# Gathering a convolution's last three rows by GpSimd, and turning them once for several tiles, in a hybrid SSD and attention layer

## The chip, the cores and the metric

The kernel runs on one core of a Trainium2 chip. The metric is the device time of one execution in microseconds (us). A core has five engines with a queue each, which is worked off in order: TensorE (PE in the profile; its weight loads are shown apart as PEld), VectorE (DVE), ScalarE (ACT), GpSimd (POOL) and SyncE (SP, which only issues DMA transfers here). ACT and POOL issue transfers as well. Engines wait for each other by semaphores.

## The reference, cut to what matters

One layer of a decoder trunk is computed for 512 prompt rows and for 8 samples of 8 rows each, 576 columns together in the kernel. After a first feed-forward block, one wide projection makes, among others, the 3072 channels `xBC`. These run through a causal depthwise convolution of four taps and SiLU, and then into the SSD scan and the attention branch's merge. Two outputs are the last three rows of the convolution's input: `conv_prompt` (3 x 3072) and `conv_sample` (8 x 3 x 3072).

```python
def causal_conv(xbc, conv_prev, conv_w, conv_b):
    L = xbc.shape[1]
    xa = jnp.concatenate([conv_prev.astype(xbc.dtype), xbc], axis=1)
    y = conv_b + sum(xa[:, j:j + L] * conv_w[j] for j in range(D_CONV))
    return jax.nn.silu(y), xa[:, L:]
```

For the prompt, `conv_prev` is zero; for the samples it comes from `state_conv`. The second value that is returned, `xa[:, L:]`, is what this document is about. The outputs are stored with a row's channels side by side, while the kernel holds channels on partitions, so that these rows have to be turned (transposed) on their way out.

## The kernel before, in words

All activations lie with 128 channels on the partitions and the 576 rows along the free dimension. Every large matrix product is made of three products of rounded halves (`mm3`, lines 207 to 215): the weights come by DMA into `stage`, ACT rounds them to `whi` (L176), and DVE or POOL subtracts to `wlo` (L177). In this part of the kernel every second subtraction goes to POOL (`share[0] = 2`). `whi` and `wlo` have four buffers, and a tile of 128 output channels uses two of each. The 576 rows are worked off in two halves of 288, each in one PSUM bank given out by `acc()`; in the convolution part that is the pool `acc` with two banks. One half is 24 matmuls of 288 columns.

`conv_tile` handles 128 of the 3072 channels. It is called 24 times, by `group_in(g)` for the four groups g: once for the group's B channels, once for C, four times for x. `group_in(0)` stands ahead of the attention branch's output projection; the groups 1 to 3 are computed beside `group_scan` of the group before, in the order that a scheduler puts the instructions in by priority and its own simulated times. `soon()` raises the priority of what is inside it.

One tile goes like this. POOL zeroes three columns of `xr` and copies the samples' old rows into it (L1156, L1157). PE computes the first half, DVE evicts it (L1161). PE computes the second half, DVE evicts its prompt columns (L1166) and its sample columns (L1168). Then PE turns the last 3 + 8 x 11 = 91 columns of `xr` into the unused columns 384 to 511 of the second half's own bank (L1174; `acc(True)` hands out the full bank), ACT copies the turned rows to `tt` (L1176), and ACT's queue issues four transfers from `tt` to the outputs: three rows of `conv_p` (L1177) and three times eight rows of `conv_s` (L1180). `tt` has one buffer.

The convolution itself is one ACT operation (L1185), three on DVE (L1187), a tanh on ACT that overwrites `xr` (L1188), and two DVE operations that write `bT`, `cT` or `xg` (L1189, L1191). `xr` has three buffers and `cv` (tag `kf`) two.

In `group_scan`, `bT` and `cT` are multiplied on PE (L1319), `xg` is turned (L1342), and `xdt` and `dk` are the operands of the scan's products (L1345, L1333, L1358). The bank tag `tr` (two banks) serves the other turns.

Of the kernel before, what the change touches and what calls it, by code (L numbers as in the profile page):

```python
# [17 lines left out]
AF = mybir.ActivationFunctionType  # L18
# [5 lines left out]
P = 128  # L24
OFFSET = 3000
D = 1024
NP = 512
NS = 64
NT = NP + NS
HT = NT // 2  # L30
B = 8
T = 8
# [3 lines left out]
CONV = 3072  # L36
# [6 lines left out]
CZ, CX, CB, CC, CDT = 0, 2048, 4096, 4608, 5120  # L43
# [46 lines left out]
def ap3(ap, offset, dims):  # L90
    return bass.AP(tensor=ap.tensor, offset=ap.offset + offset, ap=[list(d) for d in dims])


def build(ctx, tc, A, O):
    nc = tc.nc
    uid = [0]

    def tl(pool, shape, dt=F32, tag=None, bufs=None):
        uid[0] += 1
        kw = {} if bufs is None else {"bufs": bufs}  # L100
        return pool.tile(shape, dt, tag=tag, name=f"{tag}_{uid[0]}", **kw)
# [5 lines left out]
    act = nc.scalar.activation  # L107
    V = nc.vector
    G = nc.gpsimd

    constp = ctx.enter_context(pool("const"))
# [10 lines left out]
    ident = tl(constp, [P, P], tag="ident")  # L122
# [9 lines left out]
    def tr():  # L132
        return bank("tr", 2)
# [9 lines left out]
    def acc(full=False):  # L143

        wide[1] += 1
        a = wide[0]() if wide[0] and wide[1] % 2 else tl(accp, [P, 512], tag="acc")
        return a if full else a[:, :HT]
# [270 lines left out]
    with pool("h1", reuse_waits="tile") as hp:  # L418
        hts = [tl(hp, [P, NT], tag=f"h{k}") for k in range(8)]
        nrm1 = Norm(0)  # L420
        with pool("xin", side="right", reuse_waits="tile") as xi:
# [4 lines left out]
            for half in range(2):  # L426
                d = slice(half * (D // 2), (half + 1) * (D // 2))
                for c in range(5):
                    n = P if c < 4 else NS
# [5 lines left out]
            t = tr()  # L435
            nc.tensor.transpose(t[:, :8], r1, ident[:8, :8])
            V.tensor_copy(P1[:, :8], t[:, :8])
            for k in range(8):
                t = tr()
# [6 lines left out]
                t = sm()  # L446
# [5 lines left out]
            for c in range(5):  # L452
                n = P if c < 4 else NS
# [6 lines left out]
        with pool("setup2", side="right", reuse_waits="tile") as su:  # L460
            q = nc.scalar

            r1 = tl(su, [66, P], tag="r1")

            def rows(o, ap, n):
                q.dma_start(out=r1[o:o + n, :], in_=ap.rearrange("o (k p) -> (o k) p", p=P))

            rows(0, A["ffn1_norm"], 8)
            rows(8, A["mix_norm"], 8)
            rows(16, A["ffn2_norm"], 8)  # L470
            rows(24, A["ssd_norm"], 16)
            rows(40, A["conv_b"], 24)
            for i in range(2):
                q.dma_start(out=r1[64:65, i * 64:(i + 1) * 64], in_=A["q_norm"])
                q.dma_start(out=r1[65:66, i * 64:(i + 1) * 64], in_=A["k_norm"])
            t = tr()
            nc.tensor.transpose(t[:, :66], r1, ident[:66, :66])
            V.tensor_copy(P1[:, 8:], t[:, 8:66])
            V.tensor_scalar(P1[:, 40:64], t[:, 40:64], 0.5, None, ALU.mult)
            V.tensor_scalar(P1[:, 64:65], t[:, 64:65], -0.125, None, ALU.mult)  # L480
            r2 = tl(su, [96, P], tag="r2")
            q.dma_start(out=r2, in_=A["conv_w"].rearrange("o j (k p) -> (o j k) p", p=P))
            P2 = tl(constp, [P, 96], tag="P2")
            t = tr()
            nc.tensor.transpose(t[:, :96], r2, ident[:96, :96])
            V.tensor_scalar(P2, t[:, :96], 0.5, None, ALU.mult)
            r3 = tl(su, [16, 2], tag="r3")
            q.dma_start(out=r3, in_=A["d_skip"].rearrange("o (j e) -> (o j) e", e=2))
            r4 = tl(su, [16, 2, 64], tag="r4")
            V.tensor_copy(r4, r3.unsqueeze(2).to_broadcast([16, 2, 64]))  # L490
            dsk = tl(constp, [P, 16], tag="dsk")
            t = tr()
            nc.tensor.transpose(t[:, :16], r4.rearrange("j e p -> j (e p)"), ident[:16, :16])
            V.tensor_copy(dsk, t[:, :16])

            bb = tl(constp, [48, 1], tag="bb")
            behind(q.dma_start(out=bb[:32], in_=A["dt_bias"].rearrange("o h -> h o")), nrm1.insts[7])
            behind(q.dma_start(out=bb[32:48], in_=A["b_f"].rearrange("o h -> h o")), nrm1.insts[7])
            V.tensor_scalar(bb[32:48], bb[32:48], -1.0, None, ALU.mult)
            al = tl(constp, [48, 1], tag="al")  # L500
            V.memset(al, 0.0)
            behind(q.dma_start(out=al[:32], in_=A["a_log"].rearrange("o h -> h o")), nrm1.insts[7])
            act(al, al, AF.Exp)
            V.tensor_scalar(al, al, -1.0, None, ALU.mult)

            pcol = tl(su, [P, B], I32, tag="pcol")
            for b in range(B):
                q.dma_start(out=pcol[:, b:b + 1], in_=ap3(A["page_table"], b * NPG, [(1, NPG), (0, 8), (1, 1)]))
            rq = tl(su, [P, 4], tag="rq")
            q.dma_start(out=rq, in_=A["consts"][:, COFF["rq"][0]:COFF["rq"][0] + 4])  # L510
            pidx = tl(constp, [P, B, 4], I32, tag="pidx")
            pf32 = tl(su, [P, B], tag="pf32")
            V.tensor_copy(pf32, pcol)
            V.tensor_scalar(pf32, pf32, 32.0, None, ALU.mult)
            V.tensor_tensor(pidx, pf32.unsqueeze(2).to_broadcast([P, B, 4]), rq.unsqueeze(1).to_broadcast([P, B, 4]), ALU.add)
# [67 lines left out]
    win = A["w_in"][0]  # L583
# [18 lines left out]
    with pool("dtf", side="right", reuse_waits="tile") as dp:  # L602
        w = []
# [7 lines left out]
        for half in range(2):  # L611
            a = pv()
# [29 lines left out]
        for c in range(5):  # L642
            n = P if c < 4 else NS
            t = tr()
# [17 lines left out]
    with pool("att", side="right", reuse_waits="tile") as ap:  # L662
# [67 lines left out]
        for p in range(2):  # L730
            for g2 in range(0, 4, 2):
                st2 = []
                for k in range(0, 8, 4):
                    stg = tl(wp, [P, 4, 2, 2, 64], tag="stage", bufs=4)
                    for gi in range(2):
                        for e in range(2):
                            c0 = CQ + (2 * p + e) * 256 + (g2 + gi) * 64
                            nc.sync.dma_start(out=stg[:, :, gi, e, :],
                                              in_=win[k * P:(k + 4) * P, c0:c0 + 64].rearrange("(k p) c -> p k c", p=P))
# [29 lines left out]
        t = tr()  # L769
# [378 lines left out]

    XR = [P, 3 + NP + B * (T + 3)]

    def conv_tile(ct, w, prev, out):

        xr = tl(xz, XR, tag="xr", bufs=3)
        xsamp = xr[:, 3 + NP:]
        xsamp = xsamp.rearrange("p (b u) -> p b u", u=T + 3)
        G.memset(xr[:, :3], 0.0)  # L1156
        first = G.tensor_copy(xsamp[:, :, :3], prev.rearrange("p (j b) -> p b j", b=B))  # L1157
        a = acc()
        mm3(a, w, xs, 0)
        with soon():  # L1160
            V.tensor_tensor(xr[:, 3:3 + HT], a, rbc[:, hs(0)], ALU.mult)  # L1161
        a = acc(True)
        full, a = a, a[:, :HT]
        mm3(a, w, xs, 1)
        with soon():
            V.tensor_tensor(xr[:, 3 + HT:3 + NP], a[:, :NP - HT], rbc[:, HT:NP], ALU.mult)  # L1166
        with soon():
            V.tensor_tensor(xsamp[:, :, 3:], a[:, NP - HT:].rearrange("p (b t) -> p b t", t=T),  # L1168
                            rbc[:, NP:].rearrange("p (b t) -> p b t", t=T), ALU.mult)

        n = 3 + (T + 3) * B
        with soon():
            t = full[:n, 512 - P:]
            nc.tensor.transpose(t, xr[:, NP:], ident)  # L1174
            tt = tl(xz, [n, P], tag="tt", bufs=1)
            act(tt, t, AF.Copy)  # L1176
        nc.scalar.dma_start(out=O["conv_p"][0, 0, :, ct * P:(ct + 1) * P], in_=tt[:3])  # L1177
        for j in range(3):
            r = 3 + T + j
            nc.scalar.dma_start(out=O["conv_s"][0, :, j, ct * P:(ct + 1) * P], in_=tt[r:r + (T + 3) * (B - 1) + 1:T + 3])  # L1180

        m = NP + B * (T + 3)
        cv = tl(mixp, XR, tag="kf", bufs=2)
        wc = lambda j: P2[:, j * 24 + ct:j * 24 + ct + 1]
        act(cv[:, :m], xr[:, :m], AF.Identity, bias=P1[:, 40 + ct:41 + ct], scale=wc(0))  # L1185
        for j in range(1, 4):
            V.scalar_tensor_tensor(cv[:, :m], xr[:, j:j + m], wc(j), cv[:, :m], ALU.mult, ALU.add)  # L1187
        tanh = act(xr[:, :m], cv[:, :m], AF.Tanh)  # L1188
        V.scalar_tensor_tensor(out[:, :NP], xr[:, :NP], 1.0, cv[:, :NP], ALU.add, ALU.mult)  # L1189
        samples = lambda v: v[:, NP + 3:].rearrange("p (b u) -> p b u", u=T + 3)[:, :, :T]  # L1190
        last = V.scalar_tensor_tensor(out[:, NP:].rearrange("p (b t) -> p b t", t=T), samples(xr), 1.0, samples(cv), ALU.add, ALU.mult)  # L1191
        convs.append((first, tanh, last))
# [3 lines left out]
    def group_in(g):  # L1196

        scT = tl(xz, [P, 6, 24], tag="scT", bufs=1)
        nc.sync.dma_start(out=scT[:, :4, :], in_=scD[:, 4 * g:4 * g + 4, :])
        nc.sync.dma_start(out=scT[:, 4:, :], in_=ap3(scD, (16 + g) * 24, [scD.ap[0], (4 * 24, 2), (1, 24)]))  # L1200
        bT = tl(xz, [P, NT], tag="bT", bufs=2)
        conv_tile(16 + g, Cols(win, CB + g * P, width=P).get(0), scT[:, 4, :], bT)
        cT = tl(xz, [P, NT], tag="cT", bufs=2)
        conv_tile(20 + g, Cols(win, CC + g * P, width=P).get(0), scT[:, 5, :], cT)
        xc = Cols(win, CX + g * 512)
        xg = tl(xz, [P, 4, NT], tag="xg", bufs=2)
        for i in range(4):
            conv_tile(4 * g + i, xc.get(i), scT[:, i, :], xg[:, i, :])
        return bT, cT, xg

    nxt = group_in(0)
# [344 lines left out]
```

## Time and profile before

| | us |
|---|---|
| median of three runs | 1865.89 |
| lowest and highest of them | 1864.46, 1866.64 |
| the profiled execution | 1864.62 |
| its span, first to last instruction | 1862.8 |

The profile is of one execution. "Busy" is the time in which an engine had an instruction in work; the matmuls are pipelined, so that two that are started 0.13 us apart last 0.29 us each in the rows. A row of the groups or of the waits names a line of the kernel, an engine, and the tile written. A suffix q (ACTq) is the engine's queue: issuing a transfer takes the queue's time and not the engine's. A wait for several semaphores is put down to the one that came last.

### The profile page before, as it was taken

Reading aid. Unit: us, or ns where it says so; the run is one execution under the profiler, and the core shown is the slowest. Engines: PE = TensorE matmul, PEld = TensorE weight load, DVE = VectorE, ACT = ScalarE, POOL = GpSimd, SP = SyncE. Lnnn points to the kernel's source line nnn. Section 1 sums busy time; section 2 is a strip of 40 time slices with the busy share of each in tenths; the row PEclk is TensorE's granted clock in tenths of the full one; section 3 lists DMA queues with packets and bytes.
Section 4 is the critical chain, followed back from the end, with each engine's and each line's share of the span. In section 5 each row is a group of like instructions: output and inputs, shape, how many; then the busy total and the mean of one; then the engine's idle time right before and its main releaser. Section 6 shows DMA issues by size and latency. Waiting matters only on the chain.

```text
span 1862.8 us, 38777 instructions
## 1 busy us (share of the span) xinstructions
PE 1827.1 (98%) x15335; PEld 1724.5 (93%) x15335; DVE 1050.9 (56%) x2281; ACT 754.9 (41%) x1571; POOL 626.4 (34%) x697
## 2 busy tenths in 40 slices
PE   8999999999999999999999999989999999999998
PEld 7999999999889888888998898878999999999998
DVE  4643334443425777776737968787676454344542
ACT  4333223333323555555426555555433333123322
POOL 0433002212322445543324544746454222002210
PEclk9999999999999999999999999999999999999999
DMA  4644443344525688775356545354473344554342
GB/s 149 163 124 136 132 140 103 114 139 138 145 72 172 194 240 246 225 226 173 91 158 184 140 126 144 108 148 135 132 226 93 118 120 128 148 146 119 108 123 65
DMA packets 297723, 269.72 MB, mean 145 GB/s; under 512 B 55068, under 2 KB 262092, under 8 KB 297388
## 3 DMA queue, kind: packets, MB, share of 16 engines
q1 hardware_dynamic: 229712, 184.16, 35.0%
q10 hardware_dynamic: 57828, 46.10, 8.0%
q0 software_dynamic: 10000, 36.97, 6.2%
q8 instruction: 121, 1.98, 0.4%
q14 instruction: 62, 0.51, 0.1%
HBM read 223.72 MB, written 38.73 MB: 141 GB/s over the span
## 4 chain that ended last, share of the span: by engine, by line
PE 87%; DVE 6%; DMA 3%; ACT 2%; issue 1%; ACTq 1%; POOL 0%; SPq 0%; DVEq 0%; POOLq 0%
PE acc L212 16%; PE acc L213 16%; PE acc L214 16%; PE pv L213 8%; PE pv L212 8%; PE pv L214 8%; PE tr L962 2%; PE tr L949 1%; PE mm L885 1%; DMA ab<-cumD 1%; DVE kf L1187 1%; PE pv L916 1%; PE pv L1358 1%; PE mm L903 1%; PE pv L1000 1%
## 5 line engine op out<-in xcount | busy, mean ns | idle before, releaser
L176 ACT ACTIVATE whi<-stage 128x512 fp32r<-128x512 f32 (+2 forms) x474 | 294.3, 622 | 696.0 <-PE acc L213 606.3
L212 PE MATMUL acc<-xh,whi 128*128 128x288 f32 x1792 | 540.9, 302 | 9.0 <-DVE xr L1161 5.6
L213 PE MATMUL acc<-xl,whi 128*128 128x288 f32 x1792 | 531.2, 296 | 0.0
L214 PE MATMUL acc<-xh,wlo 128*128 128x288 f32 x1792 | 531.2, 297 | 0.0
L177 DVE TENSOR_TENSOR wlo<-stage,whi 128x512 fp32r<-128x512 f32 (+1 forms) x373 | 271.5, 728 | 251.4 <-ACT whi L176 242.6
L212 PEld LDWEIGHTS acc<-xh,whi 128*128 128x128 f32 x1792 | 337.7, 188 | 16.5 <-DVE xr L1161 7.9
L213 PEld LDWEIGHTS acc<-xl,whi 128*128 128x128 f32 x1792 | 337.9, 189 | 1.7 <-issue 1.4
L214 PEld LDWEIGHTS acc<-xh,wlo 128*128 128x128 f32 x1792 | 337.2, 188 | 2.1 <-issue 1.5
L348 POOL TENSOR_TENSOR u<-u,s 128x288 f32<-128x288 f32 x88 | 82.1, 934 | 436.6 <-DVE u L347 378.0
L177 POOL TENSOR_TENSOR wlo<-stage,whi 128x512 fp32r<-128x512 f32 (+1 forms) x101 | 138.8, 1375 | 265.7 <-ACT whi L176 248.8
L212 PE MATMUL pv<-xh,whi 128*128 128x288 f32 (+1 forms) x720 | 213.8, 297 | 0.0
L213 PE MATMUL pv<-xl,whi 128*128 128x288 f32 (+1 forms) x720 | 212.4, 295 | 0.0
L214 PE MATMUL pv<-xh,wlo 128*128 128x288 f32 (+1 forms) x720 | 212.0, 295 | 0.0
L213 PEld LDWEIGHTS pv<-xl,whi 128*128 128x128 f32 (+1 forms) x720 | 134.5, 187 | 1.3
L212 PEld LDWEIGHTS pv<-xh,whi 128*128 128x128 f32 (+1 forms) x720 | 134.6, 187 | 0.4
L214 PEld LDWEIGHTS pv<-xh,wlo 128*128 128x128 f32 (+1 forms) x720 | 134.5, 187 | 0.2
L212 PE MATMUL pv<-hh,whi 128*128 128x288 f32 x352 | 105.7, 300 | 0.0
L213 PE MATMUL acc<-hl,whi 128*128 128x288 f32 x352 | 104.1, 296 | 0.0
L212 PE MATMUL acc<-hh,whi 128*128 128x288 f32 x352 | 104.1, 296 | 0.0
L213 PE MATMUL pv<-hl,whi 128*128 128x288 f32 x352 | 104.1, 296 | 0.0
L214 PE MATMUL acc<-hh,wlo 128*128 128x288 f32 x352 | 104.1, 296 | 0.0
L214 PE MATMUL pv<-hh,wlo 128*128 128x288 f32 x352 | 103.8, 295 | 0.0
(366 smaller groups left out, 3601.7 us busy)
## 6 DMA issues: line engine op xcount, KB each, us to landing
stage<-in_w_in_dram SPq DMA_DIRECT2D x52, 512.0 KB
stage<-in_ffn_w_up_dram SPq DMA_DIRECT2D x44, 512.0 KB
stage<-in_ffn_w_gate_dram SPq DMA_DIRECT2D x43, 512.0 KB
stage<-in_ffn_w_down_dram SPq DMA_DIRECT2D x40, 512.0 KB
h<-in_state_ssm_dram SPq DMA_DIRECT2D x64, 256.0 KB
hTD<-hT ACTq DMA_DIRECT2D x32, 256.0 KB
pb<-pastD SPq DMA_DIRECT2D x32, 256.0 KB
ab<-cumD SPq DMA_DIRECT2D x32, 256.0 KB
```

The costliest lines, as they stand in the source:

```text
L176: act(hi, view, AF.Copy)
L177: e.tensor_tensor(lo, view, hi.bitcast(F32), ALU.subtract)
L212: mm(out, lhsT=hi, rhs=a, start=first and i == 0, stop=False)
L213: mm(out, lhsT=hi, rhs=b, start=False, stop=False)
L214: end = mm(out, lhsT=lo, rhs=a, start=False, stop=last and i == n - 1)
L348: G.tensor_tensor(u, u, sil[half], ALU.mult)
L885: mm(s[:, :n], lhsT=q, rhs=ks[2 * self.p + e][:, :n], start=hl == 0, stop=hl == 1)
L903: nc.tensor.transpose(t[:, j * P:(j + 1) * P], lt[:, j * P:(j + 1) * P], ident)
L916: mm(self.ob[o:o + 32, i * P:(i + 1) * P], lhsT=vtok[j][:, v0:v0 + 32], rhs=self.pts[e][:, j * P:(j + 1) * P], start=j == 0, stop=j == i)
L949: nc.tensor.transpose(t[:, i * P:(i + 1) * P], kk[:, i, p * P:(p + 1) * P], ident)
L962: mm(s[kv * 32:(kv + 1) * 32, :], lhsT=self.q(kv), rhs=self.kT[kv // 2], start=True, stop=True)
L1000: mm(ob[kv * 32:(kv + 1) * 32, :64], lhsT=self.pt[:, i * P + kv * 32:i * P + (kv + 1) * 32], rhs=vv[:, i, kv * 64:(kv + 1) * 64], start=jq ...
```

## The change

The turn in each tile is replaced by a gather. A new tile `tail` (one buffer, up to 108 columns of 128 partitions) takes, for each of n channel tiles, the three last prompt columns and the 24 last sample columns (three of each of the eight samples). Two copies on POOL write them, raised in priority. When the n tiles have been gathered, `store3` turns `tail` at once into a `tr` bank, ACT copies it to `tt`, and two transfers on ACT's queue write all of the n tiles' rows. Within a group n is 2 for B and C, which lie 4 x 128 channels apart in the output, and 4 for the x tiles. Over the kernel, 24 turns, 24 copies on ACT and 96 transfers become 8, 8 and 16, and 48 copies on POOL are new. The turn and the copy are no longer raised in priority. The second half's bank is taken as any other half's. In the set-up, two one-column constants, `bb` and `al`, become the two columns of one tile `ba`.

```diff
-            bb = tl(constp, [48, 1], tag="bb")
+            ba = tl(constp, [48, 2], tag="ba")
+            bb, al = ba[:, :1], ba[:, 1:]
...
-            al = tl(constp, [48, 1], tag="al")
...
+    def rows3(n):
+
+        return tl(xz, [P, 108], tag="tail", bufs=1)[:, :27 * n]
+
+    def store3(tail, n, ct, step):
+
+        t = tr()
+        nc.tensor.transpose(t[:27 * n, :P], tail, ident)
+        tt = tl(xz, [108, P], tag="tt", bufs=1)
+        act(tt[:27 * n], t[:27 * n, :P], AF.Copy)
+        for name, r0, rows in (("conv_p", 0, 3), ("conv_s", 3 * n, 24)):
+            nc.scalar.dma_start(out=ap3(O[name], ct * P, [(step * P, n), (CONV, rows), (1, P)]), in_=tt[r0:r0 + rows * n])
+
-    def conv_tile(ct, w, prev, out):
+    def conv_tile(ct, w, prev, out, last3):
...
-        a = acc(True)
-        full, a = a, a[:, :HT]
+        a = acc()
         mm3(a, w, xs, 1)
...
-        n = 3 + (T + 3) * B
+        tail, i, n = last3
         with soon():
-            t = full[:n, 512 - P:]
-            nc.tensor.transpose(t, xr[:, NP:], ident)
-            tt = tl(xz, [n, P], tag="tt", bufs=1)
-            act(tt, t, AF.Copy)
-        nc.scalar.dma_start(out=O["conv_p"][0, 0, :, ct * P:(ct + 1) * P], in_=tt[:3])
-        for j in range(3):
-            r = 3 + T + j
-            nc.scalar.dma_start(out=O["conv_s"][0, :, j, ct * P:(ct + 1) * P], in_=tt[r:r + (T + 3) * (B - 1) + 1:T + 3])
+            G.tensor_copy(tail[:, 3 * i:3 * i + 3], xr[:, NP:NP + 3])
+            G.tensor_copy(tail[:, 3 * n + 24 * i:3 * n + 24 * (i + 1)].rearrange("p (b j) -> p b j", j=3), xsamp[:, :, T:])
...
         bT = tl(xz, [P, NT], tag="bT", bufs=2)
-        conv_tile(16 + g, Cols(win, CB + g * P, width=P).get(0), scT[:, 4, :], bT)
+        tail = rows3(2)
+        conv_tile(16 + g, Cols(win, CB + g * P, width=P).get(0), scT[:, 4, :], bT, (tail, 0, 2))
         cT = tl(xz, [P, NT], tag="cT", bufs=2)
-        conv_tile(20 + g, Cols(win, CC + g * P, width=P).get(0), scT[:, 5, :], cT)
+        conv_tile(20 + g, Cols(win, CC + g * P, width=P).get(0), scT[:, 5, :], cT, (tail, 1, 2))
+        store3(tail, 2, 16 + g, 4)
         xc = Cols(win, CX + g * 512)
         xg = tl(xz, [P, 4, NT], tag="xg", bufs=2)
+        tail = rows3(4)
         for i in range(4):
-            conv_tile(4 * g + i, xc.get(i), scT[:, i, :], xg[:, i, :])
+            conv_tile(4 * g + i, xc.get(i), scT[:, i, :], xg[:, i, :], (tail, i, 4))
+        store3(tail, 4, 4 * g, 1)
```

## The prediction

> **What bounds the kernel now.** I read the page first: busy shares, then the chain that ended last.
>
> ```profile
> span 1862.8 us, 38777 instructions
> PE 1827.1 (98%) x15335; PEld 1724.5 (93%) x15335; DVE 1050.9 (56%) x2281; ACT 754.9 (41%) x1571; POOL 626.4 (34%) x697
> ...
> PE 87%; DVE 6%; DMA 3%; ACT 2%; issue 1%; ACTq 1%; POOL 0%; SPq 0%; DVEq 0%; POOLq 0%
> ```
>
> PE is busy 98% of the span and 87% of the chain, so time can only be won as PE work taken away, PE idle time closed, or PE clock regained. The windows view then says where the idle time lies; its columns are length, busy microseconds of PE, PEld, DVE, ACT and POOL, the granted clock and the DMA share.
>
> ```profile
> 0.00:885.00 885.00, 873.66 (x7918) 814.08 (x7919) 456.15 (x1097) 366.29 (x765) 272.56 (x315) 1.00 0.55 160
> 885.00:1275.00 390.00, 372.42 (x2997) 340.02 (x2996) 289.04 (x560) 197.06 (x443) 182.89 (x209) 0.99 0.49 136
> 1275.00:1862.00 587.00, 581.07 (x4425) 570.36 (x4423) 305.75 (x625) 191.59 (x363) 170.92 (x174) 1.00 0.43 129
> ```
>
> All 24 convolution tiles run from 885 to 1275 us. PE idles 390.0 - 372.4 = 17.6 us there, about half of the whole span's idle time, and only there is the clock below full. Next, whom PE waits for from 890 us to 1275 us (total, times, longest):
>
> ```profile
> PE acc L212 <- DVE xr L1161: 5.6, 6, 3.2
> PE pv L1358 <- DVE xdt L1345: 3.4, 3, 1.9
> PE acc L212 <- ACT tt L1176: 1.6, 4, 0.8
> PE mm L1319 <- DVE cT L1191: 1.4, 1, 1.4
> ...
> PE acc L1174 <- DVE xr L1168: 0.4, 1, 0.4
> ```
>
> The first and third rows, 5.6 + 1.6 = 7.2 us, are waits of an ordinary matmul for a free `acc` bank. To see why, I read the longest on three engines, PE, DVE and ACT in turn.
>
> ```profile
> 1232.52 0.29 PE L213 MATMUL acc<-xl,whi 128*128 128x288 f32 x1
> 1232.66 0.27 PE L1174 MATMUL acc<-ident,xr 128*91 128x128 f32 x1
> 1232.68 0.38 PE L214 MATMUL acc<-xh,wlo 128*128 128x288 f32 x1
> 1236.23 0.61 PE L212 MATMUL acc<-xh,whi 128*128 128x288 f32 x1 [3.17 <-DVE xr L1161]
> ```
> ```profile
> 1231.50 0.21 DVE L1168 TENSOR_TENSOR xr<-acc,rbc 128x64 f32<-128x64 f32 x1
> ...
> 1234.02 1.78 DVE L1187 SCALAR_TENSOR_TENSOR kf<-xr,P,kf 128x600 f32<-128x600 f32 x1 [1.36 <-ACT kf L1185]
> 1235.73 0.44 DVE L1161 TENSOR_TENSOR xr<-acc,rbc 128x288 f32<-128x288 f32 x1
> ```
> ```profile
> 1236.07 0.26 ACT L1176 ACTIVATE tt<-acc 91x128 f32<-91x128 f32 x1
> ```
>
> There are two `acc` banks. One was evicted for the convolution at 1231.71 (L1168), but the turn L1174 writes into the same bank, so it stays held until the copy L1176 ends at 1236.33. The other is held until L1161 ends at 1236.17. PE, done with its half by 1233.06, takes whichever comes free first. Without the turn in the bank it could have gone on at 1233.06.
>
> The stop costs a second time. Two windows behind it, and one behind the 1.90-us wait at 1043:
>
> ```profile
> 1236.00:1240.00 4.00, 3.77 (x10) 2.74 (x11) 4.00 (x8) 0.64 (x3) 1.49 (x3) 0.50 0.96 300
> 1240.00:1244.00 4.00, 4.00 (x25) 4.00 (x25) 1.71 (x5) 2.14 (x4) 0.15 (x1) 0.74 0.01 4
> ...
> 1043.00:1047.00 4.00, 3.63 (x31) 2.67 (x32) 3.80 (x9) 3.98 (x11) 2.16 (x4) 0.64 0.15 36
> ```
>
> The granted clock is 0.50 and 0.74 over eight microseconds: 4 x 0.50 + 4 x 0.26 = 3.0 us of PE work lost. The Trainium skill ("TensorE: Matmul & The Clock Gate", Part 1) puts the drop to half clock behind an idle window of some 3.4 us. The trace disagrees, since waits of 3.17 and 1.90 us were followed by it; by the rule the clock term below would be left out, and the forecast be 2.0 us later.
>
> **The change part by part.** First what goes. Times are as minimum/median/maximum ns.
>
> ```profile
> L1180 ACTq DMA_DIRECT2D out_dram<-tt x72: 645/652/755, 899.7 to 1270.0; - x72
> L1176 ACT ACTIVATE tt<-acc x24: 249/272/274, 899.1 to 1268.0; 91x128 f32<-91x128 f32 x24
> L1177 ACTq DMA_DIRECT2D out_dram<-tt x24: 255/262/293, 899.4 to 1268.3; - x24
> ```
>
> *Turns.* 24 become 8. The 270 ns of one overlap with their neighbours: above, L214 starts 0.02 us behind the turn where it would start 0.13 behind L213, so that the turn cost 0.03; elsewhere a 128-column turn is followed thus:
>
> ```profile
> 927.74 0.27 PE L1174 MATMUL acc<-ident,xr 128*91 128x128 f32 x1
> 927.85 0.27 PE L1342 MATMUL mm<-ident,xg 128*64 128x128 f32 x1
> ```
>
> that is 0.11 us. 16 x 0.03 to 0.11 = 0.5 to 1.8; I take **1.1 us**. The new ones turn fewer columns (54 and 108) but stream the same 128, so a kept turn costs the same.
>
> *Bank waits.* Every half's bank is now free after its evictions, and turns go to a `tr` bank. Ceiling 7.2. The nine shorter ones sum to 7.2 - 3.2 = 4.0; they are copy latency, nothing else stands behind most of them, and I take 3.0. Of the 3.2 I take 2.1, because DVE is behind there too (L1187 waits 1.36, then takes 1.78) and the next eviction stays late. Together **5.1 us**, from 0 to 7.2.
>
> *Clock.* If the 3.2 falls below the 1.90 that still halved the clock, 3.0 come back; I take **2.0**, from 0 to 3.0.
>
> *ACT's queue.* Copies: 16 x 0.27 = 4.4 us less. Issues: 24 x 0.26 + 72 x 0.65 = 53 us go; 16 new ones (12 or 6 rows, 96 or 48 rows) come at 0.26 to 0.65 each, 4 to 10 us. ACT isn't the bound; what reaches PE is one place:
>
> ```profile
> ACT whi L176 <- DMA out_dram<-tt: 5.9, 3, 3.2
> ```
> ```profile
> 1146.27 0.63 ACT L176 ACTIVATE whi<-stage 128x512 fp32r<-128x512 f32 x1 [3.19 <-DMA out_dram<-tt]
> 1146.29 0.65 ACTq L1180 DMA_DIRECT2D out_dram<-tt  x1
> 1146.98 0.70 ACT L1188 ACTIVATE xr<-kf 128x600 f32<-128x600 f32 x1
> ```
>
> ACT stands for 3.19 us, put down to these transfers, before the tanh L1188 that `cT` needs; then PE waits the 1.4 us for `cT` (row above). I take **0.7**, from 0 to 1.4. L1174's own wait for L1168, 0.4, goes too.
>
> Gains: 1.1 + 5.1 + 2.0 + 0.7 + 0.4 = **9.3 us** (ceiling 1.8 + 7.2 + 3.0 + 1.4 + 0.4 = 13.8).
>
> Now what is added: 48 small copies on POOL. The nearest rows are the same shape the other way round, and the operation on DVE that meets it most:
>
> ```profile
> L1157 POOL COPY xr<-scT x24: 200/360/827, 897.2 to 1253.3; 128x24 f32<-128x24 f32 x24
> ```
> ```profile
> L1187 DVE SCALAR_TENSOR_TENSOR kf<-xr,P,kf x72: 820/834/1882, 899.3 to 1269.8; 128x600 f32<-128x600 f32 x72
> ```
>
> The 24-column copy by that row is 0.20 to 0.83; the 3-column one I set at most as long. Taking 0.36 + 0.15 gives 24 x 0.51 = 12 us more on POOL, 183 of 390 before, so POOL has room. L1187's maximum is over twice its median, so DVE is stretched at times; if each gather holds DVE for its length, DVE loses up to 12 us in the stretch. DVE has 6% of the chain: 0.06 x 12 = 0.7; I take **1.0**, from 0 to 12.
>
> Two waits are new. The tanh L1188 overwrites `xr`, and now waits for the gather on POOL instead of the turn on PE; behind it on ACT stand later weight roundings, hence PE. Between L1168 and the tanh lie one L1185 and three L1187, 0.9 + 3 x 0.83 = 3.4 us, which cover a gather of 0.5 and one operation ahead of it. I count 0; uncovered, ACT's tanh would be late by up to the 1.3 us of the second row below, 31 us over 24 tiles, of which PE meets only what isn't hidden by its 6.4 us of matmuls a tile. And each of the 8 turns waits for the last gather, with PE's in-order queue behind it. POOL's queue is no fast one:
>
> ```profile
> POOL wlo L177 <- ACT whi L176: 124.1, 30, 9.1
> ```
> ```profile
> L177 POOL TENSOR_TENSOR wlo<-stage,whi x45: 1257/1292/3054, 887.5 to 1274.8; 128x512 fp32r<-128x512 f32 x45
> ```
>
> POOL stands 124.1 / 30 = 4.1 us at a time at the head of its queue for ACT, and a gather queued behind such a wait shares it. But the program's order places a turn on PE only where its input should be ready: the 24 old turns waited 0.4 us in all. I take 8 x 0.1 = **0.8**, from 0 to 8 x 1.8 = 14 (one weight subtraction of 1.3, the median of the second row, and one gather of 0.5).
>
> `tail` has one buffer: the first x gather waits for the B/C turn, a tile (48 matmuls x 0.13 = 6.4 us) earlier; that tile is the cover, and without it the wait is the one just bounded. `ba` merges two tiles of the set-up and adds no instruction: 0, long before 885 us.
>
> Sum: 9.3 - 1.0 - 0.8 = **7.5 us faster**. The profiled execution took 1864.6 us (span 1862.8 and 1.8 around it), 1.3 below the median of 1865.9. So 1857.1 in the profile's terms, **1858.4** beside the median.
>
> **The rivals.**
>
> *More is won.* ACT without 43 us of issues also shortens PE's `xdt` waits (3.4 us) and the slow clock behind the 1.90-us one (4 x 0.36 = 1.4 at least). For: both lie where ACT and DVE alternate. Against: the row names DVE. 13.8 - 1.8 + about 2 = 14 us: 1852.
>
> *The time comes back.* DVE is busy 289 of 390 us, and it is what most of the remaining waits name; a PE that comes earlier waits longer there. Then only the turns and a part of the first group's waits are kept: 1.1 + 2.0 - 1.8 = 1.3 us, 1864.6.
>
> *The lock.* Each gather stretches DVE work that is on the path: 9.3 - 12 = 2.7 us slower, 1868.6. For: L1187's 1882 ns. Against: DVE idles 101 us in the stretch. The Trainium skill ("SBUF — State Buffer", SBUF: two separate sides) says that a VectorE operation with two SBUF inputs and a GpSimd one that reads SBUF exclude each other for a whole instruction. L1187 is of that kind, and its spread agrees.
>
> *Slower: the late turn.* The last gather is queued behind a weight subtraction that waits for ACT, and PE stands at the 8 turns. At 1.8 us each 14 us come and 9.3 go, and at waits near 1.9 the clock halves again, some 3 us for one such place: 9.3 - 14 - 3 = 8 us slower, 1873.6. It decides from 9.3 / 8 = 1.2 us per turn. For: the 4.1-us stands on POOL. Against: the order puts turns late.
>
> That the change doesn't free the bank would be the second rival's result.
>
> **How the numbers follow.** Forecast 0.47, more 0.13, back again 0.22, lock 0.06, late turn 0.12. About 0.2% (3.7 us) is what a measurement of this kernel can tell from no change. Forecast and more give faster: 0.60. Back again and two thirds of the lock give same: 0.26. The rest gives slower: 0.14. The range runs from 1849 (a little below the fullest gain, for an order built anew) to 1869 (the lock, and a mild late turn); it leaves out about 0.15.
>
> **What would show it.** Right: in 885 to 1275 us, no wait of L212 for a copy of `tt`, those for L1161 under 2 us in all, the stretch's granted clock nearer 1.00 than its 0.99, PE's waits at 8 turns under 1 us, ACT's DMA issues on `tt` 16. Wrong: PE waiting for the POOL gather by over 1.2 us a turn, `xdt` or `cT` waits grown by what L212's lost, L1187's mean clearly longer, or PE idle time grown outside the stretch, since the order of all work is built anew.

## The result, and the profile after

| | before | after |
|---|---|---|
| median, us | 1865.18 | 1877.13 |
| lowest and highest, us | 1864.08, 1866.64 | 1876.23, 1878.5 |
| ratio, 95% interval | | 1.0064 [1.0047, 1.0082] |
| span of the profiled execution, us | 1862.8 | 1875.9 |

The change makes the kernel slower by 0.64%, some 12 us. The forecast was 1858.4 us in a range of 1849 to 1869.

The page of after, its span, busy shares and chain:

```profile
span 1875.9 us, 38712 instructions
...
PE 1827.0 (97%) x15319; PEld 1725.8 (92%) x15319; DVE 1036.3 (55%) x2281; ACT 752.7 (40%) x1555; POOL 639.4 (34%) x745
...
PE 89%; DVE 4%; DMA 3%; ACT 2%; issue 1%; POOL 1%; ACTq 1%; SPq 0%; DVEq 0%; POOLq 0%
```

PE is busy as long as before, although 16 turns are gone. Its idle time grew from 1862.8 - 1827.1 = 35.7 us to 1875.9 - 1827.0 = 48.9 us, which is the whole of the longer span. To see where the time went, I read three milestones: the evictions of the attention projection, of the first group's output projection, and of the last group's. Each row ends with its first and last start. Before:

```profile
L1247 DVE SCALAR_TENSOR_TENSOR sq<-kf,acc x16: 442/454/456, 939.6 to 985.5; 128x288 f32<-128x288 f32 x16
...
L1446 DVE TENSOR_TENSOR accs<-acc,ssq x16: 442/456/460, 1076.4 to 1110.8; 128x288 f32<-128x288 f32 x16
...
L1453 DVE TENSOR_TENSOR accs<-acc,accs x16: 439/448/460, 1348.5 to 1375.8; 128x288 f32<-128x288 f32 x16
```

The same lines of after, ten numbers further down in its source:

```profile
L1257 DVE SCALAR_TENSOR_TENSOR sq<-kf,acc x16: 447/454/455, 940.8 to 988.5; 128x288 f32<-128x288 f32 x16
...
L1456 DVE TENSOR_TENSOR accs<-acc,ssq x16: 440/448/458, 1089.4 to 1125.6; 128x288 f32<-128x288 f32 x16
...
L1463 DVE TENSOR_TENSOR accs<-acc,accs x16: 440/451/459, 1361.6 to 1388.9; 128x288 f32<-128x288 f32 x16
```

After is 3.0 us late when the attention projection is done, 14.8 late when the first group is, and 13.1 at the end. So 11.8 us are lost between 988 and 1126 us, in group 1's convolution beside group 0's scan. The waits of PE in after, from 885 to 1290 us:

```profile
PE acc L212 <- DVE xr L1174: 7.0, 2, 6.2
PE mm L1352 <- DVE xg L1195: 5.4, 2, 2.9
PE acc L212 <- DVE sq L1257: 5.2, 1, 5.2
PE mm L1383 <- ACT bt L1362: 2.7, 1, 2.7
PE pv L1368 <- DVE xdt L1355: 2.7, 4, 1.0
```

The ten waits for a bank that before had are gone: none for the copy of `tt` is left, no turn holds an `acc` bank any more, and the two for L1174 (L1161 before) are others. In their place stand five long ones, 2.5 to 6.2 us (the row of L1195 holds two, 2.9 and 2.5). The granted clock falls at each. Windows of after behind four of them (last three columns: granted clock, DMA share, GB/s):

```profile
942.00:946.00 4.00, 4.00 (x20) 4.00 (x20) 0.36 (x2) 0.00 (x0) 0.25 (x2) 0.57 0.71 221
...
1064.00:1069.00 5.00, 5.00 (x23) 4.83 (x22) 5.00 (x9) 2.25 (x6) 2.31 (x4) 0.57 0.28 78
1184.00:1192.00 8.00, 7.33 (x45) 4.83 (x46) 7.61 (x22) 8.00 (x24) 2.10 (x2) 0.57 0.41 132
1279.00:1287.00 8.00, 6.55 (x49) 3.94 (x51) 7.52 (x26) 5.44 (x17) 0.00 (x0) 0.57 0.40 107
```

(4 + 5 + 8 + 8) x 0.43 = 10.8 us of clock are lost there, a little less where PE was idle in them. Behind the fifth, the 2.7-us wait, the window from 1050 to 1055 us has 0.66, which adds 5 x 0.34 = 1.7. Before, it was 3.0 + 1.4 = 4.4 at two places. Matmuls at a slow clock count as busy time, so that PE's busy time doesn't show what the turns saved; the two weren't taken apart.

**The longest wait, followed back.** It starts at the turn. Four engines of after between 1015 and 1064 us; first PE:

```profile
1055.39 0.60 PE L1431 MATMUL tr<-ident,hst 128*128 128x128 f32 x4
...
1057.02 0.27 PE L1158 MATMUL tr<-ident,tail 128*54 128x128 f32 x1
1063.48 0.61 PE L212 MATMUL acc<-xh,whi 128*128 128x288 f32 x1 [6.19 <-DVE xr L1174]
```

POOL, the last gather of C and the first of x:

```profile
1015.67 0.20 POOL L1186 COPY tail<-xr 128x24 f32<-128x24 f32 x1
...
1058.33 0.18 POOL L1185 COPY tail<-xr 128x3 f32<-128x3 f32 x1
```

ACT:

```profile
1059.65 1.30 ACT L1194 ACTIVATE xr<-kf 128x600 f32<-128x600 f32 x2 [0.99 <-POOL tail L1186]
```

DVE:

```profile
1056.26 0.61 DVE L1422 TENSOR_TENSOR xdt<-tr,xdt 128x64 f32<-128x64 f32 x4
1060.38 1.27 DVE L1195 SCALAR_TENSOR_TENSOR xg<-xr,kf 128x512 f32<-128x512 f32 x1 [3.51 <-ACT xr L1194]
...
1062.98 0.45 DVE L1174 TENSOR_TENSOR xr<-acc,rbc 128x288 f32<-128x288 f32 x1
```

B and C were gathered by 1015.87, but the turn comes at 1057.02, 41.1 us later, 0.15 us behind L1422 (1056.87). L1422 is what reads the `tr` bank of group 0's last scan step, in which `oo` was turned. The other seven turns come 0.1 to 3.9 us behind their gathers. Until the turn has read `tail`, no x tile can be gathered; the tanh L1194 may not overwrite an ungathered `xr` (ACT's queue also issued the turn's two transfers from 1058.17 to 1059.60, just ahead of it, so that its 0.99 us may be theirs in part); L1195 waits for the tanh; with the three `xr` buffers held, the next eviction L1174 waits; and PE waits 6.19 us for that.

**Theory A**, then: banks of one tag are given out in the order in which the program asks for them, whatever its priority. `store3` asks for a `tr` bank behind group 0's scan, and so gets one only when that scan gives one of its last two back; before, the turn had its tile's own bank and stood in no line. **Theory B:** the 48 copies on POOL hold DVE or come late. **Theory C:** the time is lost at the groups' ends, where PE has run out of other work. A fourth, that one order of instructions is luckier than another, came later.

### The profile page after: what moved, and what is told of

It is laid out like the page before. It is cut to its first block, busy times and chain, and to the rows that moved or that the text cites. A ratio compares the mean times of both kernels' runs of the same rounds, so it can differ in the third digit from the quotient of the medians.

```text
span 1875.9 us, 38712 instructions
## 1 busy us (share of the span) xinstructions
PE 1827.0 (97%) x15319; PEld 1725.8 (92%) x15319; DVE 1036.3 (55%) x2281; ACT 752.7 (40%) x1555; POOL 639.4 (34%) x745
## 4 chain that ended last, share of the span: by engine, by line
PE 89%; DVE 4%; DMA 3%; ACT 2%; issue 1%; POOL 1%; ACTq 1%; SPq 0%; DVEq 0%; POOLq 0%
PE acc L212 17%; PE acc L213 16%; PE acc L214 16%; PE pv L212 8%; PE pv L213 8%; PE pv L214 8%; PE tr L962 2%; PE tr L949 1%; PE mm L885 1%; DMA ab<-cumD 1%; PE pv L1368 1%; PE pv L916 1%; DVE kf L1193 1%; PE mm L903 1%; PE pv L1000 1%
```

## The experiments

Each time is the median beside the runs of before on the same chip (1862.2 to 1864.8 us there), so that ratios are what to compare. Two variants have no run: a second buffer for `tail`, and the new turn raised in priority while it stays in `tr`. What they would give is not shown.

| run | us | ratio, 95% interval |
|---|---|---|
| own_bank | 1861.91 | 0.9982 [0.9971, 0.9993] |
| before_gather | 1860.15 | 0.9981 [0.9971, 0.999] |
| no_bc | 1865.22 | 1.001 [0.9998, 1.0022] |
| acc_bank | 1875.39 | 1.0068 [1.005, 1.0085] |
| no_x | 1858.34 | 0.9974 [0.9963, 0.9985] |
| mm_bank | 1885.28 | 1.0116 [1.009, 1.0142] |
| after_dve | 1873.9 | 1.0057 [1.0038, 1.0076] |
| own_bank_dve | 1862.16 | 1.0004 [0.9992, 1.0015] |
| th_act | 1872.29 | 1.0044 [1.0028, 1.0059] |
| one_tail_ms | 1875.47 | 1.0059 [1.004, 1.0077] |
| before_ms | 1864.26 | 0.9997 [0.9983, 1.001] |
| own_th | 1864.26 | 0.9989 [0.9973, 1.0005] |
| acc_bank_dve | 1872.15 | 1.0057 [1.0038, 1.0076] |
| bc_own | 1867.32 | 1.0018 [1.0007, 1.0028] |
| own_share3 | 1848.75 | 0.9923 [0.9907, 0.994] |
| before_share3 | 1861.47 | 0.9981 [0.9968, 0.9994] |
| after_share3 | 1868.09 | 1.0022 [1.001, 1.0034] |
| own_share4 | 1851.94 | 0.9931 [0.9913, 0.995] |

### The turn's bank

**own_bank.** The turn goes into the last tile's own bank, and it and its copy are raised in priority, as they were before.

```diff
-        t = tr()
-        nc.tensor.transpose(t[:27 * n, :P], tail, ident)
+        with soon():
+            t = full[:27 * n, 512 - P:]
+            nc.tensor.transpose(t, tail, ident)
...
```

> After, but each of the 8 turns writes into the unused columns of the last tile's own second-half bank, raised in priority, as the 24 turns of before did. Theory A (the tr bank: banks of a tag are given in program order, so the B/C turn of group 1 waits for the scan of group 0 to give its last tr bank back; the one tail buffer then holds the x gathers, and these the tanh): the B/C turn of group 1 comes within 10 us of its last gather instead of 42, the 6.2 and 2.7 us waits of PE between 1049 and 1064 us fall under 2 together, and the time is 1860 to 1869 us. Theory B (the copies on POOL hold DVE or come late): still 1873 to 1879. Theory C (the time is lost at the ends of groups, where PE has no other work left): 1871 to 1877, with the waits of 5.3 at 941, 2.9 at 1182 and 2.5 at 1280 us kept.

It is faster than after by 0.8%, as theory A forecast, and than before by 0.18%. The turn of group 1 comes 0.1 us behind its last gather. The five long waits are gone; what PE waits for now, from 885 to 1290 us, is mostly POOL:

```profile
PE acc L1159 <- POOL tail L1188: 5.0, 4, 2.7
PE tr L264 <- POOL ssq L1299: 3.7, 2, 1.9
PE mm L266 <- POOL ssq L1299: 2.4, 1, 2.4
```

The longest of these is the prediction's late turn, and POOL's own rows show why it is late:

```profile
1000.97 4.89 POOL L177 TENSOR_TENSOR wlo<-stage,whi 128x512 fp32r<-128x512 f32 x1 [6.27 <-ACT whi L176]
1005.83 1.80 POOL L1349 TENSOR_TENSOR ab<-ab,cT 128x512 f32<-128x512 f32 x1
1007.58 0.65 POOL L1187 COPY tail<-xr 128x3 f32<-128x3 f32 x1
1008.17 0.20 POOL L1188 COPY tail<-xr 128x24 f32<-128x24 f32 x1
```

The gather stands behind a weight subtraction that waited 6.27 us for ACT and then took 4.89, and one more operation; PE stood 2.69 us at the turn. The median of these subtractions on POOL is 1.30 us in own_bank between 885 and 1275 us. Whether the long one is the prediction's lock, seen from POOL's side, no run tests.

**mm_bank.** `t = sm()` in place of `t = tr()`: a bank of the scan's other tag.

> After, with the turn in a bank of the tag mm, which the scan also uses all along. Theory A: it queues behind the scan's banks in program order too, the turn of group 1 stays over 25 us late: 1868 to 1878 us. If the tag tr alone is the matter: 1858 to 1867 us.

Slower still than after, and 7 us beyond theory A's range; why, is open. The turn of group 1 starts at 1053.4 us, its last gather ended at 1018.9: 34.5 us. So it isn't the tag `tr` alone: a bank of the scan's other tag comes late too.

**acc_bank.** `t = acc(True)`: a bank of its own from the convolution's pool.

> After, with the turn in a bank of its own from the acc pool instead of tr. Theory A: the bank given is that after the last tile's second half, free early, so the B/C turn of group 1 comes early too: 1861 to 1870 us, a little behind own_bank's gain since a turn now takes a turn of the two acc banks. Theory B: 1873 to 1879. Theory C: 1871 to 1877.

The turns come 0.1 to 1.0 us behind their gathers, as theory A wants, but the time missed what it forecast; it lies in the ranges of theories B and C. PE stands at them instead:

```profile
PE acc L1158 <- POOL tail L1186: 13.5, 7, 3.2
```

**acc_bank_dve** has the gathers on DVE besides, and was to tell whether POOL is to blame for that.

> acc_bank with the 48 gathering copies on DVE. If acc_bank was slow because PE stood at its early turns for POOL (13.5 us at 7 turns): those waits fall under 3 us and the time to 1860 to 1867 us. If the extra turn of the two acc banks is what costs: 1870 to 1877 us.

It isn't. PE still stands at the turns:

```profile
PE acc L1158 <- DVE tail L1186: 10.9, 5, 3.6
```

A turn that takes its own place in the line of the two `acc` banks has the next half behind it, so PE can't fill the time between the eviction and the gather with that half's matmuls. In own_bank the next half has the other bank and can go first: seven of its matmuls stand ahead of the turn at 1008.43 us, and none ahead of acc_bank's at 1012.12.

**no_bc** leaves out `store3(tail, 2, 16 + g, 4)`.

> After, with the turn, the copy and the two transfers of B and C left out (their rows of the two outputs are not written); the gathers stay. Theory A: nothing holds the x gathers of group 1 any more, 1859 to 1868 us. Theory B: 1873 to 1878 us. Theory C: 1871 to 1877 us.

**no_x** gathers only where `n == 2` and leaves out `store3(tail, 4, 4 * g, 1)`.

> After, with the x tiles' gathers, turns, copies and transfers left out (their rows of the two outputs are not written); B and C keep theirs, in a tr bank. Theory A in two links: (1) the B/C turn of group 1 gets its tr bank only at the end of the scan of group 0, (2) the x gathers wait for it, since tail has one buffer. Without x gathers the turn is as late as before but nothing hangs on it: the turn of group 1 over 30 us behind its gather, no PE wait over 3 us between 1040 and 1070 us, 1858 to 1868 us. If a late turn costs by itself: 1871 to 1878 us.

Without the B/C turn the time is that of before. Without the x gathers it is below before, although the B/C turn of group 1 is as late as in after: it starts at 1055.4 us, its gather ended at 1011.4, 44.0 us earlier. No wait of PE between 1040 and 1070 us passes 0.6 us. So a late turn costs nothing that can be seen by itself; what hangs on it does. The two runs together show both links of theory A, the late bank and the gathers that wait for it. How much time the second is worth no_x doesn't say, since it also leaves out the x turns and their transfers.

**bc_own** gives only the B/C turn its last tile's own bank (`t = full[:, 512 - P:] if n == 2 else tr()`).

> After, with only the B/C turn in its last tile's own bank; the x turns stay in tr. Theory A: only the B/C turn has x gathers behind it, so this alone brings the loss back: 1858 to 1867 us. If the x turns in tr cost too: 1868 to 1875 us.

It falls between the two ranges: of the 0.64% of after, 0.18% stay. The turn isn't raised in priority there and still comes 0.1 us behind its last gather (1010.40 against 1010.35 us), so that the bank alone does that. The x turns in `tr` cost too, so theory A was not complete. After's own rows show what they do; PE at the end of group 2's convolution, and the first eviction of group 1's output projection (its operands are `ygh` and `ygl`), in after and then in own_bank:

```profile
1174.13 0.29 PE L212 MATMUL acc<-ygh,whi 128*128 128x288 f32 x1
...
1177.49 0.29 PE L214 MATMUL acc<-ygh,wlo 128*128 128x288 f32 x1
...
1178.06 0.27 PE L1158 MATMUL tr<-ident,tail 128*108 128x128 f32 x1
1178.16 1.02 PE L264 MATMUL tr<-ssq,cst 128*128 128x512 f32 x2
1182.11 0.44 PE L1352 MATMUL mm<-ident,xg 128*128 128x128 f32 x2 [2.92 <-DVE xg L1195]
...
1190.59 0.61 PE L212 MATMUL acc<-ygh,whi 128*128 128x288 f32 x1
```
```profile
1189.33 0.82 DVE L1459 TENSOR_TENSOR u<-acc,ssq 128x288 f32<-128x288 f32 x2
```
```profile
1169.06 0.46 DVE L1462 TENSOR_TENSOR u<-acc,ssq 128x288 f32<-128x288 f32 x1 [0.40 <-PE acc L214]
```

L264 is the row scaling with which `group_out` of the group before begins, and it asks for its `tr` bank behind the x turn. It starts 0.1 us behind the turn, at 1178.2 and again at 1276.0 in after, 1167.8 and 1267.2 in bc_own; in own_bank, where the turns stand in no line, it starts at 1137.0 and 1234.5, 34 and 30 us ahead of the x turns. The projection itself begins at the end of the next convolution in both, at 1174.1 us in after and 1167.3 in own_bank. But in own_bank the scaling is ready, and the first half is evicted as soon as it is done. In after, two halves fill both `acc` banks by 1177.8, the scaling and with it the first eviction come at 1189.3, and the third half starts at 1190.6; from its first matmul to its last, group 1's projection takes 51.7 us against 37.5 in own_bank. In between PE had only the scan, and stood 2.9 and 2.5 us at the groups' ends. Theory C saw the right place and took the symptom for the cause. In no_x, with no x turn, L264 starts at 1139.8.

### The copies on POOL

**before_gather** adds the two copies to each tile of before, into a `tail` that nothing reads (and has after's `ba` in the set-up).

```diff
+        tail = tl(xz, [P, 108], tag="tail", bufs=1)
+        with soon():
+            G.tensor_copy(tail[:, :3], xr[:, NP:NP + 3])
+            G.tensor_copy(tail[:, 12:36].rearrange("p (b j) -> p b j", j=3), xsamp[:, :, T:])
```

> Before, with the two gathering copies on POOL added to each tile into a tile that nothing reads; the 24 turns, copies and 96 transfers stay. Theory A: POOL's copies alone cost little, 1864 to 1868 us. Theory B: they carry the loss, 1872 to 1878 us. Theory C: as A.

The added work doesn't slow the kernel; it came out 0.19% faster, below the range given, in a slightly other order. That is as much as own_bank is ahead of before, so that own_bank's 0.18% is no proof of a gain by the change. Of theory B, that the copies hold DVE falls; that they come late, this run can't tell, since nothing waits for them.

**after_dve** is after with `V.tensor_copy` for `G.tensor_copy`.

> After, with the 48 gathering copies on DVE instead of POOL. Theory A: the bank is as late as before, 1868 to 1879 us. Theory B (copies late on POOL): 1857 to 1866 us.

As slow as after: the turn of group 1 is 44.6 us behind its gather (1051.3 against 1006.8 us) with POOL out of it, and the rest of theory B falls. The turn of group 2 waits 1.40 us for L1422 by the profile, so that it is the `tr` bank that holds it there.

**own_bank_dve** has the same edit in own_bank.

> own_bank (turn in the last tile's own bank, raised in priority), with the 48 copies on DVE. PE's 5.0 us of waits for the last gather at 4 turns should fall under 1.5 us, and the time be 1855 to 1862 us; if DVE's added work (48 copies of 0.1 to 0.2 us) reaches the path instead: 1862 to 1868 us.

The turns' waits fall from 5.0 to 2.0 us, short of the 1.5 expected, but the scan's waits for DVE grow, nothing is won, and the time lies in the second reading's range:

```profile
PE pv L1371 <- DVE xdt L1358: 5.2, 3, 2.3
PE mm L1355 <- DVE xg L1199: 4.0, 4, 1.5
PE pv L1371 <- DVE dk L1346: 3.1, 2, 2.9
```

### The wait at 941 us, and the luck of an order

In after, PE and SP at the start of the attention projection:

```profile
941.40 0.58 PE L212 MATMUL acc<-yh,whi 128*128 128x288 f32 x1 [5.25 <-DVE sq L1257]
```
```profile
933.13 1.96 SPq L1245 DMA_DIRECT2D stage<-in_w_attn_proj_dram  x3
935.20 0.54 SPq L1239 DMA_DIRECT2D kf<-thD  x1
```

PE came to this place some 3 us sooner than before, but the load of `th`, which the eviction needs, was issued no sooner, behind three weight loads.

**th_act** issues that first load from ACT's queue: `(nc.sync if j else nc.scalar).dma_start(out=th, ...)`.

> After, with the attention projection's first load of th issued by ACT's queue instead of SP's, where it stood behind weight loads. If the 5.3 us wait at 941 us (and the half clock behind it) comes from that queue: the wait falls under 2 us and the time to 1868 to 1874 us. If the load waits for its buffer anyway: 1874 to 1879 us. Theory A says nothing on it; the waits at 1050 and 1063 us stay in both.

The wait is 2.1 us instead of 5.3, a little over the 2 expected, and the time is inside the first reading's range. Its interval overlaps that of after, so that the 0.2% between them, some 4 us, are likely and not settled. **own_th**, the same in own_bank, was to win little, and won nothing: it lies at the border of its two readings, and its interval overlaps own_bank's.

> own_bank with the first load of th on ACT's queue. That wait of PE was 0.6 us in own_bank, so little is left to win: 1858 to 1864 us; if ACT's queue, where the load now waits for its buffer, holds the weight roundings: 1864 to 1868 us.

**one_tail_ms** and **before_ms** merge two one-column tiles of the attention part, in after and in before.

```diff
-                    mn = tl(tp, [P, 1], tag="mn", bufs=4)
+                    ms = tl(tp, [P, 2], tag="mn", bufs=4)
+                    mn, sum_ = ms[:, :1], ms[:, 1:]
...
-                    sum_ = tl(tp, [P, 1], tag="sum", bufs=4)
```

> After, with two one-column tiles of the attention part (mn and sum) made the columns of one: the same work on every engine, another order. It measures what an order alone is worth here. Theory A: the turn of group 1 is late in this order too, 1871 to 1882 us. If after's loss is the luck of one order: anything from 1858 to 1870 us.

> Before, with the same two tiles merged: the same work, another order. Its distance from before is the size of that luck: expected within 5 us of 1865, 1860 to 1869 us.

Both times stay: 1.0059 as after, 0.9997 as before. But the merge hardly made another order: by the traces, at most 8 of 15319 matmuls stand at another place in one_tail_ms, 10 of 15335 in before_ms, and none of DVE's or POOL's operations. So these two runs show how well a time repeats, and nothing on an order's luck. What speaks against luck are after_dve and after_share3: 1502 and 1645 matmuls stand elsewhere than in after, the turn of group 1 is late all the same, and they are slower (1.0057 and 1.0022) than own_bank_dve and own_share3 (1.0004 and 0.9923). That is two orders, and not many.

### What own_bank still waits for

**own_share3** and **own_share4** give POOL every third or fourth weight subtraction (`share[0] = 3`, `4`) in own_bank; **before_share3** and **after_share3** have every third in before and after.

> own_bank with every third weight subtraction on POOL instead of every second, from the mixing part on. If own_bank is held by POOL's late results (5.0 us at turns, 6.1 us for ssq): those fall and the time is 1854 to 1861 us; if DVE, which takes them over at 0.7 us each, is the bound: 1861 to 1869 us.

> own_bank with every fourth subtraction on POOL. If DVE has room left: 1844 to 1849 us; if DVE becomes the bound: 1850 to 1858 us.

> Before, with every third weight subtraction on POOL instead of every second. If POOL's lateness holds before as well: 1852 to 1860 us, and own_share3's 1848.8 stays a few us ahead by the freed banks; if the share alone makes own_share3's gain: 1846 to 1851 us; if it helps only with the gathers on POOL: 1862 to 1868 us.

> After, with every third weight subtraction on POOL. The turns in tr stay late whoever subtracts: 10 to 20 us behind own_share3, 1859 to 1869 us, with the turn of group 1 over 25 us behind its last gather. If the lateness came from POOL: 1847 to 1855 us.

own_share3 is the fastest kernel of the study, 0.77% faster than before and well below what was expected of it. Its row for the turns:

```profile
PE acc L1159 <- POOL tail L1188: 6.1, 5, 3.2
```

So half of my reason was wrong: the turns' waits for POOL did not fall (6.1 after 5.0). The waits for `ssq` did; none of the 6.1 us is left among PE's waits. The two parts give more together than apart: the share alone 0.19%, the bank alone 0.18%, both 0.77%. What of it is the free banks' and what POOL's is not taken apart. before_share3 falls between the ranges of its readings. own_share4 lies within own_share3's interval, and in the range for a DVE that has become the bound; its own waits weren't followed. after_share3 is slower than before and its turn of group 1 is 40.4 us behind its gather (1045.5 against 1005.1 us): the line at the bank stays whoever subtracts.

## Why the prediction was wrong

**The step that failed** is the part on `tail`: "the first x gather waits for the B/C turn, a tile (48 matmuls x 0.13 = 6.4 us) earlier; that tile is the cover". In group 1 the turn came 41.1 us after its gather, not within a tile (in the other groups the cover held, 0.3 to 2.2 us), because "turns go to a `tr` bank" was costed at nothing. I looked at what the `acc` bank would gain by losing the turn, and not at the line that the turn joined, nor at who stands behind it there: the x gathers by the one `tail` buffer, and the row scaling by the next `tr` bank. What stood behind it cost PE a wait of 6.19 us at the late turn, and 2.92 and 2.51 us at the groups' ends, each with a slow clock behind it. The order argument ("the program's order places a turn on PE only where its input should be ready") held for the input and left the bank out.

Point by point:

- **Bank waits** (5.1 us): right about the copy of `tt`, for which PE waits nowhere in after. The sign that the waits for L1161, now L1174, would fall under 2 us in all failed: they are 7.0 us, 6.2 of them behind the late turn.
- **Clock** (2.0 us won): wrong in sign. The place at 1236 us was mended, but five long waits came, and 10.8 + 1.7 = 12.5 us of clock were lost behind them, against 4.4 in before.
- **Turns** (1.1 us): can't be read by itself; PE's busy time is 1827.0 after 1827.1, with the slower clock in it.
- **ACT's queue** (0.7 us): right; the wait for `cT` is gone. The 16 issues took a median of 679 ns, 10.9 us in all, a little over the 4 to 10 forecast.
- **The copies on POOL** (1.0 us lost): mis-sized, on the safe side. Their rows:

```profile
L1185 POOL COPY tail<-xr x24: 179/186/1141, 898.3 to 1274.4; 128x3 f32<-128x3 f32 x24
L1186 POOL COPY tail<-xr x24: 197/204/829, 898.4 to 1275.0; 128x24 f32<-128x24 f32 x24
```

24 x (0.19 + 0.20) = 9.4 us by the medians, against 12; L1193 (L1187 before) has a mean of 937 ns between 885 and 1290 us after 952, where the lock would have made it longer, and before_gather shows no loss. DVE shows no sign of the lock.

- **The new turns' waits** (0.8 us lost): near 0 in after, where the turns are too late to wait. As soon as they are early, the late turn is there: 5.0 us in own_bank, 13.5 in acc_bank. That rival's mechanism was real, and its 4.1-us stands on POOL were the right row, but in this kernel another took its place. It gave the right side, slower, with the wrong cause.
- **The time comes back**: it did at the attention projection, where PE was 3 us early and left 3 us late, and in part in own_bank_dve.

## What to carry to other kernels

When an operation is moved to another buffer or bank, ask who asked for that tag ahead of it and who asks behind it: in these runs the line was kept in the program's order, and a piece of filler put into the line of a long phase inherits the end of that phase. A single buffer that is filled again needs its reader to be prompt; if the reader stands in such a line, everything that may not overwrite the buffer's source stands with it. And a long wait of TensorE costs more than its length: by the windows above, the five of 2.5 to 6.2 us in after lost another 1.7 to 3.4 us of clock each.

## What was unexpected of the hardware

The granted clock fell to half behind waits of 2.51 us (1279.6 us in after) and, in before, of 1.90 us, while waits of 1.44 us (before, 1149 us) did not do it. The length of one wait doesn't decide it: 1.77 us in no_x (1024.9 us) was followed by a clock of 0.50, while 1.78 us in after (1029.4 us) and 1.97 us in before_share3 (1038.2 us) left it at 1.00. Work added on an engine with room can leave the time lower: before_gather, with 48 copies more on POOL, ran 0.19% faster than before.
